# Gated linear attention in blocks of 128 tokens, and two heads or maps at a time in the softmax and stick-breaking attentions

## The chip, the core and the metric

The kernel runs on one core of one Trainium2 chip. The metric is the device time of one execution in microseconds (us); the median of several is given. A core has five engines with their own instruction streams: TensorE (PE, matrix products), VectorE (DVE), ScalarE (ACT), GpSimd (POOL) and SyncE (SP, which starts most transfers here). They wait for each other by semaphores. PE's clock is granted at one of two levels, 1.2 and 2.4 GHz; the profile gives the mean grant of a stretch as a share of the higher one.

## What is computed

Two network blocks in a chain, on 512 tokens of width 1024, all in float32. The first (two layers) has stick-breaking attention (8 heads of 64), differential attention (4 heads, two maps of 64 each), a mixture of experts and a gate. The second has a gated delta network, a gated linear attention, a merge and a lookup of single experts. What the change touches:

```python
def stick_breaking_attention(q, k, v):            # per head, per block of 128 queries
    z = einsum('bhqd,bhkd->bhqk', qb, k) * scale
    strict = key_idx[None, :] < q_idx[:, None]
    log_stay = where(strict, log_sigmoid(-z), 0.0)
    between = cumsum(log_stay, axis=3, reverse=True) - log_stay
    w = where(strict, exp(log_sigmoid(z) + between), 0.0)
    return einsum('bhqk,bhkd->bhqd', w, v)

def differential_attention(q, k, v, lam):         # two maps m per head
    s = einsum('bhmqd,bhmkd->bhmqk', qb, k) * scale
    a = softmax(where(allowed, s, neg), axis=-1)
    return einsum('bhqk,bhkd->bhqd', a[:, :, 0] - lam * a[:, :, 1], v)

def _gla_chunked(q, k, v, logf, s0):              # chunks of 64 tokens; run forwards and backwards
    bc = cumsum(logf, axis=3)
    ref = bc[..., CHUNK // 2:CHUNK // 2 + 1, :]
    scores = einsum('bhnid,bhnjd->bhnij', q * exp(bc - ref), k * exp(ref - bc))
    scores = where(incl, scores, 0.0)
    o_intra = einsum('bhnij,bhnjv->bhniv', scores, v)
    q_dec = q * exp(bc)
    k_dec = k * exp(bc[..., -1:, :] - bc)
    tot = exp(bc[..., -1, :])
    def step(S, xs):
        qd_c, kd_c, v_c, tot_c = xs
        o_c = einsum('bhcd,bhdv->bhcv', qd_c, S)
        S = tot_c[..., :, None] * S + einsum('bhcd,bhcv->bhdv', kd_c, v_c)
        return S, o_c
    s_fin, o_inter = scan(step, s0, (q_dec, k_dec, v, tot))
    return o_intra + o_inter, s_fin
```

The gated linear attention has 8 heads of 128, runs over 256 context tokens first (4 chunks, only the state counts) and then over the 512 tokens (8 chunks), in both directions, and is normed and gated.

## The kernel before

Tiles are 128 partitions by up to 512 columns. PE multiplies a weight tile (rows of weights are contracted, columns of weights become rows of the result) with a moving tile and writes into a bank of 128x512 fp32 in PSUM. A weight tile of 64 rows takes half of the array's rows, one of 64 columns half of its columns. A plain fp32 product runs as two passes, a transpose (against `ident`) as one. Projections by large weights (`proj`, `proj2`) are made of three products of split numbers each (`mm3`, L305 to L311: hi x hi, hi x lo, lo x hi), into `acc`, `acc2` or `acc_c`; the split of a raw weight tile into `w_hi` (ACT) and `w_lo` (DVE or POOL) is L291 to L293 and L1212 to L1213.

The program is written in Python loops; a list scheduler then fixes each engine's order ahead of the run, so products of different steps stand mixed on PE, in an order that does not change at run time. How many tiles of a name live at once is set by pools: `bufs=1` makes the next user wait for the last reader.

*stick* (L566) goes through 8 heads; per head and block of keys `kb` it makes the logits `z` (L581: 64 weight rows, 128 to 512 columns), adds a mask by a product with `ident_b` (L582), takes softplus on ACT and DVE, splits it into `sp_hi` and `sp_lo`, sums over later keys by products with triangles (L597), takes exp into `st_w` and multiplies with `v` into `po` (L601: 64 weight columns; two heads share a bank). *diff* (L609) makes logits `s` (L630, mask L631) of the two maps one after the other, softmax, difference, transposes and `ydif` (L649). Projections of the same layer fill PE between them.

*gla* (L1628) works on four groups `hg` of two heads. It projects q, the two forget gates and v of a group (`proj2`), then per head `j` and direction `d`:

- a cumulative sum `bc` (L1709) of the log gates, in place; `x` and `e1`, the scaled k and q (L1712 to L1719);
- scores of each of 8 chunks into one bank per head that a product with zeros (`zb`, L1702) has cleared: later queries against all 64 keys (L1725), earlier queries against the earlier 32 (L1727); so 16 products a direction, with 32 moving columns each;
- `qd`, `kd`, the totals, and `kd` transposed into `kn` (L1744, copied out by ACT at L1745);
- per chunk in order, 11 of 12 chunks, the state product `kv` (L1758: 64 weight rows, into `pt_kv0` or `pt_kv1` by the chunk's half of its block of 128), and the state update on DVE (L1765, L1767) into `S8`;
- after both directions, a multiply with a mask `le` (L1770), a sum of directions on POOL (L1772), and per chunk three products into `gl_o` (L1776: scores with v; L1777 and L1778: `qd` with the state of each direction), each with 64 weight columns. Then norm, gate, transposes (`pt_o`, L1793) and a split.

The gate projection of a group (`g_ev`) is issued in its first head, the merge gates' projection (`between(hg)`) behind its second. PSUM in this stage: four banks for `acc`, two for `pt`, two for `tr` (`pt_s`, `gl_o`).

Of the kernel before, what the change touches and what calls it, by code (L numbers as in the profile page):

```python
# [20 lines left out]
P = 128  # L21
D = 1024
S = 512
NB = S // P
# [154 lines left out]
class Net:  # L179
# [386 lines left out]
    def stick(self, qT, kT, v, op, pool):  # L566

        nc = self.nc
        res = []
        po = None  # L570
        for h in range(8):
            t, r0 = h // 2, (h % 2) * 64
            rows = slice(r0, r0 + 64)
            if h % 2 == 0:
                po = self.tr("po")
                nc.tensor.matmul(po, self.zero_b[:, :P], self.zero_b, start=True, stop=True)
            sp = [None] * 4
            for kb in (3, 2, 1, 0):
                n = S - kb * P
                z = self.pt("z")[:, :n]  # L580
                nc.tensor.matmul(z, kT[t][rows, kb * P:(kb + 1) * P], qT[t][rows, kb * P:], start=True, stop=False)  # L581
                nc.tensor.matmul(z[:, :P], self.ident_b, self.mask_sb, start=False, stop=True)  # L582
                e = pool.tile([P, S], F32, tag="st_e", name="st_e")[:, :n]
                nc.scalar.activation(out=e, in_=z, func=AF.Abs)
                nc.scalar.activation(out=e, in_=e, func=AF.Exp, scale=-1.0)
                nc.scalar.activation(out=e, in_=e, func=AF.Ln, bias=1.0)
                f = pool.tile([P, S], F32, tag="st_f", name="st_f")[:, :n]
                nc.vector.scalar_tensor_tensor(f, z, 0.0, e, op0=ALU.max, op1=ALU.add)
                hi = pool.tile([P, n], F32R, tag=f"sp_hi{kb}", name="sp_hi")
                lo = pool.tile([P, n], F32R, tag=f"sp_lo{kb}", name="sp_lo")  # L590
                nc.vector.tensor_copy(hi, f)
                nc.vector.tensor_tensor(lo, f, hi.bitcast(F32), op=ALU.subtract)
                sp[kb] = (hi, lo)
                for k2 in range(kb, 4):
                    tri = self.neg_tri if k2 == kb else self.neg_ones
                    for part in range(2):
                        nc.tensor.matmul(z[:, (k2 - kb) * P:], tri, sp[k2][part], start=False,  # L597
                                         stop=True, skip_group_check=True)
                w = pool.tile([P, S], F32, tag="st_w", name="st_w")[:, :n]
                nc.scalar.activation(out=w, in_=z, func=AF.Exp)  # L600
                nc.tensor.matmul(po[rows, kb * P:], v[kb][:, h * 64:(h + 1) * 64], w, start=False,  # L601
                                 stop=True, skip_group_check=True)
            if h % 2 == 1:
                o = op.tile([P, S], F32, tag=f"oa{t}", name=f"oa{t}")
                nc.scalar.copy(o, po)
                res.append(o)
        return res

    def diff(self, i, dn, dv, ap, op, pool, steps):  # L609

        nc = self.nc
# [9 lines left out]
        res = []  # L621
        for h in range(4):
            y = self.tr("ydif")
            for qb in range(NB):
                n = (qb + 1) * P
                es = []
                for m in range(2):
                    rows = slice(64 * m, 64 * m + 64)
                    s = self.pt("s")[:, :n]
                    nc.tensor.matmul(s, T["q"][h][rows, qb * P:(qb + 1) * P], T["k"][h][rows, :n], start=True, stop=False)  # L630
                    nc.tensor.matmul(s[:, n - P:], self.ident_b, self.mask_da, start=False, stop=True)  # L631
                    mx = self.tiny.tile([P, 1], F32, tag=f"mx{m}", name="mx")
# [473 lines left out]
    def masks2(self):  # L1106
# [11 lines left out]

        self.le2 = c.tile([P, 2, P], F32, name="le2")
# [164 lines left out]
    def gdn(self, acts, gp, oa_d):  # L1284
        nc = self.nc
        self.conv = gp.tile([P, 24, 3], F32, name="conv")
# [341 lines left out]
    def gla(self, acts, keep, between):  # L1628
# [8 lines left out]
        with ExitStack() as st:  # L1637
# [6 lines left out]
            zb = gp.tile([P, 1, P], BF16, name="zb2")  # L1644
            nc.gpsimd.memset(zb, 0.0)
            res = []
            for hg in range(4):
# [50 lines left out]
                for j in range(2):  # L1698
                    h = hg * 2 + j
                    Sst, qd = [], []  # L1700
                    sps = self.tr("pt_s")
                    nc.tensor.matmul(sps.rearrange("p (n i) -> p n i", n=4), zb[:, 0], zb.to_broadcast([P, 4, P]),  # L1702
                                     start=True, stop=True)
                    sps = sps.rearrange("p (d b i) -> p d b i", d=2, b=NB)
                    for d in range(2):
# [666 lines left out]
```

## Time and profile before

| | us |
|---|---|
| median of 3 runs | 4505.92 (4497.12 to 4510.54) |
| profiled execution, its own time | 4499.69 |
| its span on the core | 4497.9 |
| PE busy, 21636 instructions | 4207.5 |
| DVE busy | 2759.6 |
| ACT busy | 1669.0 |
| POOL busy | 1137.9 |

The profile is of one execution, on the profiler's clock. Busy times of PE are of pipelined products: a product's shown duration overlaps with its neighbours, so the price of one is read from the distance between starts. Rows of "busy time by stretch" are: start:end, length, then PE, weight load (PEld), DVE, ACT and POOL with busy us and instruction counts, then PE's granted clock, the busy share of the transfer engines and GB/s. Rows by operation give line, engine, operation, output<-inputs, weight rows*columns, moving rows x columns, count, busy time, mean duration in ns, and the idle time before it with what ended most of it. The GLA runs from about 2303 to 2954 us; the attentions of the two layers from about 95 to 345 and from about 905 to 1190 us.

### The profile page before, as it was taken

To read this page: it belongs to the slowest core of one execution; us is meant where nothing else is said; L and a number is where in the kernel's file an instruction comes from. 1 tells how busy PE (TensorE), PEld (TensorE's weight loads), DVE (VectorE), ACT (ScalarE), POOL (GpSimd) and SP (SyncE) were. 2 spreads that over 40 slices of the span, in tenths; PEclk is the share of its full clock that TensorE was granted. 3 is DMA by queue.
4 is the path that set the end of the run, shared out by engine and by line. 5 is a ranking of instruction groups with operands and counts; after the bars stand their busy time and mean duration, and the time that the engine had idled before them with its cause. 6 is when DMAs were issued, how large, how long until landed. Compare 5 with 4: busy or idle time off the path is not lost. (4 is left out here: it accounts for less than half of the span.)

```text
span 4497.9 us, 59856 instructions
## 1 busy us (share of the span) xinstructions
PE 4207.5 (94%) x21636; PEld 3209.9 (71%) x21637; DVE 2759.6 (61%) x6172; ACT 1669.0 (37%) x3160; POOL 1137.9 (25%) x1086
## 2 busy tenths in 40 slices
PE   8999899999989998889999999998889999999998
PEld 6677544767764466777877676676779888988986
DVE  5455455544554564778753544534999777777776
ACT  4544211454421154444433232323346433333333
POOL 2002100100020023222000110214679534343443
PEclk9999999999999998899988898999999999999999
DMA  4144796313459921222211111124135898888875
GB/s 131 36 125 152 287 419 253 112 50 96 131 202 410 411 76 54 53 63 62 62 29 40 31 50 40 38 89 152 59 115 202 278 317 304 294 300 304 286 271 197
DMA packets 342590, 739.77 MB, mean 164 GB/s; under 512 B 72512, under 2 KB 175024, under 8 KB 314640
## 3 DMA queue, kind: packets, MB, share of 16 engines
q1 hardware_dynamic: 277536, 540.54, 36.0%
q0 software_dynamic: 45376, 167.76, 10.2%
q10 hardware_dynamic: 19376, 27.57, 1.7%
q8 instruction: 174, 2.85, 0.3%
q14 instruction: 128, 1.05, 0.1%
HBM read 694.07 MB, written 41.70 MB: 164 GB/s over the span
## 5 line engine op out<-in xcount | busy, mean ns | idle before, releaser
L308 PE MATMUL acc<-rn_hi,w_hi 128*128 128x512 f32 x1224 | 520.4, 426 | 34.3 <-ACT w_hi L1212 16.2
L308 PE MATMUL acc<-rn_hi,w_lo 128*128 128x512 f32 x1224 | 517.9, 424 | 31.5 <-DVE w_lo L1213 12.2
L308 PE MATMUL acc<-rn_lo,w_hi 128*128 128x512 f32 x1224 | 513.3, 419 | 2.0 <-POOL rn_lo L275 2.0
L293 POOL TENSOR_TENSOR w_lo<-w_raw,w_hi 128x512 fp32r<-128x512 f32 x103 | 136.1, 1322 | 1035.5 <-ACT w_hi L291 922.9
L2195 ACT CAST p_hi<-p_raw 128x1024 fp32r<-128x1024 f32 x256 | 268.5, 1049 | 330.9 <-PE pu L308 243.1
L291 ACT CAST w_hi<-w_raw 128x512 fp32r<-128x512 f32 x316 | 196.1, 621 | 516.3 <-PE acc L308 400.0
L308 PE MATMUL pu<-rn_hi,p_lo 128*128 128x384 f32 x1024 | 352.0, 344 | 16.8 <-POOL p_lo L2196 14.4
L308 PE MATMUL pu<-rn_hi,p_hi 128*128 128x384 f32 x1024 | 349.8, 342 | 4.6 <-ACT p_hi L2195 3.5
L308 PE MATMUL pu<-rn_lo,p_hi 128*128 128x384 f32 x1024 | 349.0, 341 | 0.0
L2196 DVE TENSOR_TENSOR p_lo<-p_raw,p_hi 128x1024 fp32r<-128x1024 f32 x243 | 297.1, 1223 | 72.7 <-ACT p_hi L2195 72.7
L293 DVE TENSOR_TENSOR w_lo<-w_raw,w_hi 128x512 fp32r<-128x512 f32 x213 | 151.4, 711 | 272.7 <-ACT w_hi L291 261.4
L308 PEld LDWEIGHTS acc<-rn_hi,w_lo 128*128 128x128 f32 x1224 | 243.5, 199 | 103.7 <-DVE w_lo L1213 16.7
L308 PE MATMUL py<-p_hi,ahi 128*128 128x512 f32 x768 | 304.7, 397 | 6.3 <-ACT ahi L274 3.8
L308 PE MATMUL py<-p_lo,ahi 128*128 128x512 f32 x768 | 304.8, 397 | 1.3 <-DVE p_lo L2196 1.3
L308 PE MATMUL py<-p_hi,alo 128*128 128x512 f32 x768 | 304.9, 397 | 0.0
L308 PEld LDWEIGHTS acc<-rn_hi,w_hi 128*128 128x128 f32 x1224 | 242.5, 198 | 86.3 <-ACT w_hi L1212 19.7
L308 PEld LDWEIGHTS acc<-rn_lo,w_hi 128*128 128x128 f32 x1224 | 242.5, 198 | 44.6 <-issue 4.2
L2185 POOL DMA_INDIRECT eu<-in_expert_v_dram,idx x128 | 189.0, 1477 | 266.9 <-DVE py L2089 250.5
L2185 POOL DMA_INDIRECT eu<-in_expert_u_dram,idx x128 | 179.2, 1400 | 281.7 <-DVE dots L2075 264.4
L956 PE MATMUL gu<-wgu,xe 128*64 128x512 f32 x1024 | 243.3, 600 | 0.0
L308 PEld LDWEIGHTS pu<-rn_hi,p_lo 128*128 128x128 f32 x1024 | 194.8, 190 | 23.6 <-POOL p_lo L2196 17.9
L308 PEld LDWEIGHTS pu<-rn_hi,p_hi 128*128 128x128 f32 x1024 | 195.0, 190 | 10.4 <-ACT p_hi L2195 4.7
(736 smaller groups left out, 9609.2 us busy)
## 6 DMA issues: line engine op xcount, KB each, us to landing
w_raw<-in_w_in_dram SPq DMA_DIRECT2D x336, 256.0 KB, 2.7
p_raw<-in_expert_u_T_dram SPq DMA_DIRECT2D x128, 512.0 KB, 3.6
p_raw<-in_expert_v_dram SPq DMA_DIRECT2D x128, 512.0 KB, 4.9
wgu<-in_w_exp_gate_dram SPq DMA_DIRECT2D x62, 1024.0 KB, 11.8
wgu<-in_w_exp_up_dram SPq DMA_DIRECT2D x62, 1024.0 KB, 14.0
wdn<-in_w_exp_down_dram SPq DMA_DIRECT2D x60, 1024.0 KB, 12.2
ada_w<-in_w_ada_dram SPq DMA_DIRECT2D x96, 256.0 KB, 3.0
gates_d<-gst ACTq DMA_DIRECT2D x24, 1024.0 KB, 4.3
```

The lines of the kernel that those rows point to most:

```text
L291: self.nc.scalar.copy(hi, raw)
L293: eng.tensor_tensor(lo, raw, hi.bitcast(F32), op=ALU.subtract)
L308: self.nc.tensor.matmul(ps, l, r, start=st, stop=sp or shared, skip_group_check=shared)
L956: nc.tensor.matmul(gu[64 * e:64 * e + 64, :], xe[:, c, 64 * e:64 * e + 64], wgu[e][:, :, c, :], start=c == 0, stop=c == KC - 1)
L2185: self.nc.gpsimd.indirect_dma_start(out=t, out_offset=None, in_=rows, in_offset=bass.IndirectOffsetOnAxis(ap=idx, axis=0))
L2195: self.nc.scalar.copy(hi, raw)
L2196: (eng or self.nc.vector).tensor_tensor(lo, raw, hi.bitcast(F32), op=ALU.subtract)
```

## The change

The stick attention takes two heads at a time: both `z` products, both masks, then softplus and weights of each, then both `po`. The differential attention issues the `s` products of both maps together. Four masks that only the delta network uses are built at its start (`masks_gdn`). In the gated linear attention work goes by blocks of 128 tokens (two chunks): scores of a block are two products with 128 weight columns and 2x32 moving columns (the earlier half of keys from `xh`, a shifted copy of `x` in which other places hold values that are not used), and a copy by a mask of integers (`inside`) takes the diagonal 64x64 parts into `sc`, which stays zero elsewhere; `kn` holds each chunk's keys with zeros in the other chunk's rows, so a state product has 128 weight rows, and four share one bank `pt_kv`; the products of scores with v have 128 weight rows and columns, and the products with the states follow, first one column half, then the other.

```diff
@@ stick @@
+        for t in range(4):
+            po = self.tr("po")
...
+                zs = [self.pt("z")[:, :n] for _ in halves]
+                for z, rows in zip(zs, halves):
+                    nc.tensor.matmul(z, kT[t][rows, kb * P:(kb + 1) * P], qT[t][rows, kb * P:], start=True, stop=False)
+                for z in zs:
+                    nc.tensor.matmul(z[:, :P], self.ident_b, self.mask_sb, start=False, stop=True)
...
+                    sp[r][kb] = (hi, lo)
...
+                for r, rows in enumerate(halves):
+                    h = 2 * t + r
+                    nc.tensor.matmul(po[rows, kb * P:], v[kb][:, h * 64:(h + 1) * 64], ws[r], start=False,
+                                     stop=True, skip_group_check=True)
@@ diff @@
-                for m in range(2):
+                both = [self.pt("s")[:, :n] for _ in range(2)]
+                for m, s in enumerate(both):
                     rows = slice(64 * m, 64 * m + 64)
-                    s = self.pt("s")[:, :n]
                     nc.tensor.matmul(s, T["q"][h][rows, qb * P:(qb + 1) * P], T["k"][h][rows, :n], start=True, stop=False)
+                for s in both:
                     nc.tensor.matmul(s[:, n - P:], self.ident_b, self.mask_da, start=False, stop=True)
@@ gla @@
-            zb = gp.tile([P, 1, P], BF16, name="zb2")
-            nc.gpsimd.memset(zb, 0.0)
+            inside = gp.tile([P, 2, P], I32, name="inside")
...
+            sc = gp.tile([P, 2, NB, P], F32, name="gl_sc")
+            kn = gp.tile([P, 6, 2, P], F32, name="gl_kn")
+            xh = gp.tile([P, 32 + 8 * 64], F32, name="gl_xh")
+            for t in (sc, kn, xh):
+                nc.gpsimd.memset(t, 0.0)
...
-                        for c in range(8):
-                            p0 = 64 * (c % 2)
-                            nc.tensor.matmul(sps[p0:p0 + 64, d, c // 2, ilate], x[:, c, :], e1[:, c, ilate],
-                                             start=False, stop=True, skip_group_check=True)
-                            nc.tensor.matmul(sps[p0 + early.start:p0 + early.stop, d, c // 2, early], x[:, c, early],
-                                             e1[:, c, early], start=False, stop=True, skip_group_check=True)
+                        nc.vector.tensor_copy(xh[:, 32:].rearrange("p (c i) -> p c i", c=8)[:, :, 0:32], x[:, :, early])
+                        xf = xh[:, 32 - early.start:][:, :S]
+                        sps = self.tr("pt_s").rearrange("p (b i) -> p b i", b=NB)
+                        for b in range(NB):
+                            cs = slice(2 * b, 2 * b + 2)
+                            s2 = sps[:, b].rearrange("p (c i) -> p c i", c=2)
+                            nc.tensor.matmul(s2[:, :, ilate], x[:, cs].rearrange("p c i -> p (c i)"), e1[:, cs, ilate],
+                                             start=True, stop=True)
+                            nc.tensor.matmul(s2[:, :, early], xf[:, b * P:(b + 1) * P], e1[:, cs, early],
+                                             start=True, stop=True)
+                        nc.vector.copy_predicated(out=sc[:, d], mask=inside[:, d:d + 1].to_broadcast([P, NB, P]), data=sps)
...
+                        ends = tp.tile([P, 12, 1], F32, tag="ends", name="gl_ends", bufs=1)
+                        nc.vector.tensor_copy(ends, bc[:, :, last:last + 1])
...
+                        kd = bc
...
-                            nc.scalar.copy(kn[:, b0:b0 + nb], pt[:, :nb * P].rearrange("p (b c) -> p b c", c=P))
+                            for hf in range(2):
+                                nc.scalar.copy(kn[H[hf], b0:b0 + nb, hf], pt[H[hf], :nb * P].rearrange("p (b c) -> p b c", c=P))
...
-                                nc.tensor.matmul(pt[:, n * P:(n + 1) * P], kn[cs, c // 2, :], v[cs, c // 2, j * P:(j + 1) * P],
-                                                 start=True, stop=True)
+                                nc.tensor.matmul(kv, kn[:, c // 2, c % 2, :], v[:, c // 2, j * P:(j + 1) * P], start=True, stop=True)
...
-                    tt(sc, sps, self.le.unsqueeze(2).to_broadcast([P, 2, NB, 64]), op=ALU.mult)
-                    ss = tp.tile([P, NB, 64], F32, tag="scs", name="gl_scs", bufs=1)
+                    ss = tp.tile([P, 768], F32, tag="vT", name="gl_scs", bufs=1)[:, :512].rearrange("p (b i) -> p b i", b=NB)
...
-                    for c in range(8):
-                        cs, b = H[c % 2], c // 2
-                        nc.tensor.matmul(o[cs, b, :], ss[cs, b, :], v[cs, b, j * P:(j + 1) * P], start=True, stop=False)
-                        nc.tensor.matmul(o[cs, b, :], qd[0][:, c, :], Sst[0][:, c, :], start=False, stop=False)
-                        nc.tensor.matmul(o[cs, b, :], qd[1][:, c, :], Sst[1][:, c, :], start=False, stop=True)
+                    for b in range(NB):
+                        nc.tensor.matmul(o[:, b, :], ss[:, b, :], v[:, b, j * P:(j + 1) * P], start=b == 0, stop=True, skip_group_check=True)
+                    for b in range(NB):
+                        for d in range(2):
+                            for c in (2 * b, 2 * b + 1):
+                                nc.tensor.matmul(o[H[c % 2], b, :], qd[d][:, c, :], Sst[d][:, c, :], start=False, stop=True,
+                                                 skip_group_check=True)
```

The scheduler's order on PE, in the first heads phase of the GLA. State products of the second direction of the first head before the change (`acc` are projection products, `pt_kv` state products; numbers behind names tell tiles apart):

```order
L308 MATMUL acc_20574<-rn_hi_13383,w_hi_20597 128x512
L1758 MATMUL pt_kv1_20206<-glv_19923,gl_kn_20182 128x128
L308 MATMUL acc_20574<-rn_lo_13384,w_hi_20597 128x512
L308 MATMUL acc_20574<-rn_hi_13383,w_lo_20598 128x512
L308 MATMUL acc_20575<-rn_hi_13383,w_hi_20597 128x512
L308 MATMUL acc_20575<-rn_lo_13384,w_hi_20597 128x512
L1758 MATMUL pt_kv0_20205<-glv_19923,gl_kn_20182 128x128
L308 MATMUL acc_20575<-rn_hi_13383,w_lo_20598 128x512
L1758 MATMUL pt_kv1_20206<-glv_19923,gl_kn_20182 128x128
L308 MATMUL acc_20576<-rn_hi_13383,w_hi_20597 128x512
```

and after it:

```order
L1782 MATMUL pt_kv_20199<-glv_19931,gl_kn_19572 128x128
L308 MATMUL acc_20537<-rn_hi_13371,w_lo_20562 128x512
L308 MATMUL acc_20538<-rn_hi_13371,w_hi_20561 128x512
L1782 MATMUL pt_kv_20190<-glv_19931,gl_kn_19572 128x128
L308 MATMUL acc_20538<-rn_lo_13372,w_hi_20561 128x512
L308 MATMUL acc_20538<-rn_hi_13371,w_lo_20562 128x512
L308 MATMUL acc_20539<-rn_hi_13371,w_hi_20561 128x512
L1782 MATMUL pt_kv_20190<-glv_19931,gl_kn_19572 128x128
L308 MATMUL acc_20539<-rn_lo_13372,w_hi_20561 128x512
```

Each state product now writes a bank shared by four, and stands alone among projection products as most did before; with 128 weight rows its place in a row half is gone.

Scores of the second direction of the first head before (L1725 later queries, L1727 earlier ones; sixteen in all, one state product among them):

```order
L1758 MATMUL pt_kv1_20122<-glv_19923,gl_kn_20108 128x128
L1725 MATMUL pt_s_20073<-gl_e1_20152,gl_x_20150 64x32
L1727 MATMUL pt_s_20073<-gl_e1_20152,gl_x_20150 32x32
L1725 MATMUL pt_s_20073<-gl_e1_20152,gl_x_20150 64x32
L1727 MATMUL pt_s_20073<-gl_e1_20152,gl_x_20150 32x32
L1725 MATMUL pt_s_20073<-gl_e1_20152,gl_x_20150 64x32
L1727 MATMUL pt_s_20073<-gl_e1_20152,gl_x_20150 32x32
```

and after, with both directions of the head next to each other (L1747 and L1749):

```order
L308 MATMUL acc2_20260<-rn_hi_13371,w_lo_20282 128x512
L1749 MATMUL pt_s_20090<-gl_e1_20084,gl_xh_19573 128x2x32
L1747 MATMUL pt_s_20090<-gl_e1_20084,gl_x_20082 128x2x32
L1749 MATMUL pt_s_20090<-gl_e1_20084,gl_xh_19573 128x2x32
L1747 MATMUL pt_s_20090<-gl_e1_20084,gl_x_20082 128x2x32
L1749 MATMUL pt_s_20090<-gl_e1_20084,gl_xh_19573 128x2x32
L1747 MATMUL pt_s_20090<-gl_e1_20084,gl_x_20082 128x2x32
L1749 MATMUL pt_s_20090<-gl_e1_20084,gl_xh_19573 128x2x32
L1747 MATMUL pt_s_20157<-gl_e1_20151,gl_x_20149 128x2x32
L308 MATMUL acc2_20259<-rn_hi_13371,w_hi_20299 128x512
```

Sixteen small products became eight, and transposes of `kd` and projections stand between the sets.

Outputs of the first head before (L1776 scores with v, L1777 and L1778 the states):

```order
L308 MATMUL acc_20574<-rn_hi_13383,w_lo_20616 128x512
L1778 MATMUL gl_o_20227<-gl_S_20193,gl_qd_20173 64x128
L1776 MATMUL gl_o_20227<-glv_19923,gl_scs_20225 64x128
L1777 MATMUL gl_o_20227<-gl_S_20119,gl_qd_20099 64x128
L1778 MATMUL gl_o_20227<-gl_S_20193,gl_qd_20173 64x128
L1776 MATMUL gl_o_20227<-glv_19923,gl_scs_20225 64x128
L1777 MATMUL gl_o_20227<-gl_S_20119,gl_qd_20099 64x128
L1778 MATMUL gl_o_20227<-gl_S_20193,gl_qd_20173 64x128
```

and after (L1795 scores with v, L1799 the states; x2 are two products on the two column halves):

```order
L1795 MATMUL gl_o_20217<-glv_19931,gl_scs_20215 128x128 x4
...
L308 MATMUL acc_20539<-rn_hi_13371,w_lo_20598 128x512
L1799 MATMUL gl_o_20217<-gl_S_20189,gl_qd_20167 64x128 x2
L1799 MATMUL gl_o_20217<-gl_S_20122,gl_qd_20100 64x128 x2
L1799 MATMUL gl_o_20217<-gl_S_20189,gl_qd_20167 64x128 x2
L1799 MATMUL gl_o_20217<-gl_S_20122,gl_qd_20100 64x128 x2
L1799 MATMUL gl_o_20217<-gl_S_20189,gl_qd_20167 64x128 x2
```

The four full products stand some eighty rows ahead of the run of products with the states, which alternates between the column halves; before, three products in turn wrote the same half.

## Rows read from the trace of the kernel before

**Rows 1.** The page: busy time of each engine, share of the span, instructions.

```profile
PE 4207.5 (94%) x21636; PEld 3209.9 (71%) x21637; DVE 2759.6 (61%) x6172; ACT 1669.0 (37%) x3160; POOL 1137.9 (25%) x1086
```

**Rows 2.** Busy time by stretch, stick and diff (columns as said above).

```profile
95.00:240.00 145.00, 144.63 (x633) 95.06 (x632) 55.82 (x129) 76.47 (x171) 7.86 (x7) 1.00 0.18 50
...
1050.00:1190.00 140.00, 136.27 (x635) 98.50 (x634) 83.19 (x198) 61.01 (x140) 10.36 (x8) 0.99 0.44 119
```

**Rows 3.** The same view, the GLA whole and three stretches of it.

```profile
2303.80:2953.90 650.10, 616.88 (x2993) 439.24 (x2993) 301.01 (x527) 192.77 (x300) 90.41 (x60) 0.88 0.14 39
...
2303.00:2428.00 125.00, 119.04 (x517) 78.42 (x517) 60.53 (x118) 31.55 (x52) 15.44 (x12) 0.78 0.11 32
2428.00:2494.00 66.00, 59.84 (x316) 50.56 (x314) 32.67 (x33) 28.93 (x42) 15.21 (x8) 0.95 0.21 56
...
2858.00:2954.00 96.00, 93.19 (x487) 61.58 (x488) 46.06 (x103) 20.95 (x36) 9.77 (x8) 0.95 0.11 31
```

**Rows 4.** The same view, one heads phase cut at its runs.

```profile
2358.80:2365.70 6.90, 6.90 (x45) 4.36 (x44) 0.00 (x0) 0.03 (x1) 0.00 (x0) 1.00 0.05 16
2375.60:2378.90 3.30, 3.30 (x34) 2.64 (x33) 1.64 (x3) 1.57 (x4) 1.28 (x1) 1.00 0.03 11
2379.00:2382.30 3.30, 3.30 (x13) 2.17 (x14) 0.32 (x2) 0.89 (x2) 1.27 (x1) 0.50 0.00 0
...
2385.80:2406.20 20.40, 20.40 (x53) 12.30 (x52) 5.79 (x13) 2.09 (x4) 0.73 (x1) 0.50 0.05 13
```

**Rows 5.** The same view, first and last of the four group borders.

```profile
2298.00:2314.00 16.00, 8.30 (x30) 5.70 (x29) 15.55 (x18) 8.73 (x14) 7.42 (x7) 0.68 0.11 44
...
2836.00:2847.00 11.00, 5.51 (x23) 4.22 (x22) 11.00 (x8) 6.72 (x12) 10.31 (x6) 0.69 0.15 36
```

**Rows 6.** PE by operation and shape in the GLA (xcount | busy, mean).

```profile
L1758 PE MATMUL pt_kv<-glv,gl_kn 64*128 64x128 f32 x352 | 86.1, 367 | 0.0
...
L1702 PE MATMUL pt_s<-zb 128*128 128x512 bf16 x8 | 3.6, 447 | 1.2 <-DVE g_gt L1595 1.2
```

**Rows 7.** Timeline of PE, kv alone (start, duration, operation, passes).

```profile
2354.04 0.50 PE L308 MATMUL acc<-rn_hi,w_hi 128*128 128x512 f32 x1
2354.47 0.48 PE L1758 MATMUL pt_kv<-glv,gl_kn 64*128 64x128 f32 x2
2354.89 0.50 PE L308 MATMUL acc<-rn_lo,w_hi 128*128 128x512 f32 x1
```

**Rows 8.** Timeline of PE, four 128x128 products, then projections.

```profile
270.08 1.08 PE L649 MATMUL ydif<-dv,da_t 128*128 128x128 f32 x8
270.92 0.48 PE L308 MATMUL acc<-rn_hi,w_lo 128*128 128x512 f32 x1
271.23 0.39 PE L308 MATMUL acc<-rn_hi,w_hi 128*128 128x512 f32 x1
271.46 0.39 PE L308 MATMUL acc<-rn_lo,w_hi 128*128 128x512 f32 x1
```

**Rows 9.** Timeline of PE, one 128x128 product alone, and the next.

```profile
249.45 0.49 PE L649 MATMUL ydif<-dv,da_t 128*128 128x128 f32 x2
249.78 0.22 PE L631 MATMUL s<-mask_da,ident_b 128*128 128x128 bf16 x1
```

**Rows 10.** Timeline of PE, two kv in different row halves.

```profile
2348.84 0.49 PE L1758 MATMUL pt_kv<-glv,gl_kn 64*128 64x128 f32 x4
```

**Rows 11.** Timeline of PE, po of two heads together, of one alone.

```profile
114.49 1.07 PE L601 MATMUL po<-st_w,v 128*64 128x512 f32 x4
...
126.98 1.07 PE L601 MATMUL po<-st_w,v 128*64 128x512 f32 x2
```

**Rows 12.** DVE by operation and shape in the GLA.

```profile
L1767 DVE SCALAR_TENSOR_TENSOR gl_S<-gl_S,gl_tot,pt_kv 128x128 f32<-128x128 f32 x112 | 38.8, 346 | 71.5 <-PE pt_kv L1758 70.7
...
L1770 DVE TENSOR_TENSOR gl_sc<-pt_s,le 128x512 f32<-128x512 f32 x8 | 5.5, 691 | 27.8 <-PE pt_s L1727 27.8
```

**Rows 13.** Waits of PE in the GLA (us in total, times, longest).

```profile
PE pt_o L1793 <- DVE gl_y L1788: 8.4, 4, 2.2
```

More of the change, by code (lines that the diff above doesn't have):

```diff
@@ L569, in stick @@
         res = []
[L570 to L577, printed above, removed]
+        halves = (slice(0, 64), slice(64, 128))
+        for t in range(4):
+            po = self.tr("po")
+            nc.tensor.matmul(po, self.zero_b[:, :P], self.zero_b, start=True, stop=True)
+            sp = [[None] * 4 for _ in halves]
@@ L578, in stick @@
             for kb in (3, 2, 1, 0):
                 n = S - kb * P
[L580 to L600, printed above, removed]
@@ new lines, in stick @@
+                for z in zs:
+                    nc.tensor.matmul(z[:, :P], self.ident_b, self.mask_sb, start=False, stop=True)
+                ws = []
+                for r, z in enumerate(zs):
+                    e = pool.tile([P, S], F32, tag="st_e", name="st_e")[:, :n]
+                    nc.scalar.activation(out=e, in_=z, func=AF.Abs)
+                    nc.scalar.activation(out=e, in_=e, func=AF.Exp, scale=-1.0)
+                    nc.scalar.activation(out=e, in_=e, func=AF.Ln, bias=1.0)
+                    f = pool.tile([P, S], F32, tag="st_f", name="st_f")[:, :n]
+                    nc.vector.scalar_tensor_tensor(f, z, 0.0, e, op0=ALU.max, op1=ALU.add)
+                    hi = pool.tile([P, n], F32R, tag=f"sp_hi{kb}", name="sp_hi")
+                    lo = pool.tile([P, n], F32R, tag=f"sp_lo{kb}", name="sp_lo")
+                    nc.vector.tensor_copy(hi, f)
+                    nc.vector.tensor_tensor(lo, f, hi.bitcast(F32), op=ALU.subtract)
+                    sp[r][kb] = (hi, lo)
+                    for k2 in range(kb, 4):
+                        tri = self.neg_tri if k2 == kb else self.neg_ones
+                        for part in range(2):
+                            nc.tensor.matmul(z[:, (k2 - kb) * P:], tri, sp[r][k2][part], start=False,
+                                             stop=True, skip_group_check=True)
+                    w = pool.tile([P, S], F32, tag="st_w", name="st_w", bufs=3)[:, :n]
+                    nc.scalar.activation(out=w, in_=z, func=AF.Exp)
+                    ws.append(w)
@@ L607, in stick @@
+                for r, rows in enumerate(halves):
+                    h = 2 * t + r
+                    nc.tensor.matmul(po[rows, kb * P:], v[kb][:, h * 64:(h + 1) * 64], ws[r], start=False,
+                                     stop=True, skip_group_check=True)
+            o = op.tile([P, S], F32, tag=f"oa{t}", name=f"oa{t}")
+            nc.scalar.copy(o, po)
+            res.append(o)
         return res
@@ L626, in diff @@
                 es = []
-                for m in range(2):
+                both = [self.pt("s")[:, :n] for _ in range(2)]
+                for m, s in enumerate(both):
                     rows = slice(64 * m, 64 * m + 64)
-                    s = self.pt("s")[:, :n]
                     nc.tensor.matmul(s, T["q"][h][rows, qb * P:(qb + 1) * P], T["k"][h][rows, :n], start=True, stop=False)
+                for s in both:
                     nc.tensor.matmul(s[:, n - P:], self.ident_b, self.mask_da, start=False, stop=True)
+                for m, s in enumerate(both):
                     mx = self.tiny.tile([P, 1], F32, tag=f"mx{m}", name="mx")
@@ L1117, in masks2, with masks_gdn @@
                                         base=0, channel_multiplier=-sgn)
+    def masks_gdn(self, c):
+        nc = self.nc
         self.le2 = c.tile([P, 2, P], F32, name="le2")
```

35 lines of the change are left out of this document (11 added, 24 removed).

## Prediction

> **What bounds the kernel now.** I read the page's busy shares first: TensorE (PE) works 94% of the span [rows 1], so a change pays where PE has less to do or stops less. Busy times by stretch then separate the two places that the change touches. In the stick-breaking and differential attentions PE is busy 144.63 of 145 us and 136.27 of 140, at granted clock 1.00 and 0.99, with VectorE (DVE) and ScalarE (ACT) at 83 us or less [rows 2]: those are plain sums of PE work. The gated linear attention (GLA) is the long one: 650.1 us from its first projection to its last transpose, PE busy 616.88, mean granted clock 0.88 [rows 3]. It alternates: four heads phases (125, 107, 107 and 96 us, 435 together), in which the small products of two heads run between projection products, and three stretches of pure projection (66, 75 and 75 us, clock 0.95).
>
> Where the clock falls is seen in one heads phase cut fine [rows 4]. During a run of output products it is 1.00, during a run of sixteen score products too, but just behind such a run it is 0.50 (the lower of the two levels, 1.2 of 2.4 GHz), for 3.3 us once and for 20.4 us the next time. What else is low lies at the four group borders, three of 11 us and one of 16, at 0.68 to 0.69 with PE busy about half [rows 5]: there PE waits for split weights.
>
> So the GLA's 650.1 us split into 33.2 us of idle PE (650.10 less 616.88), a loss to the clock of 0.12 x 650 = 78 us (156 us at the lower level, each losing half), and 539 us of work at full clock. Of the 156 us, the 49 us of border at about 0.685 make 31; some 125 are left, which I put down to the score runs.
>
> **The change part by part.** An fp32 product is two PE passes in the trace (x2 is one product).
>
> *State products (kv).* 352 passes, 176 products, with 64 rows of weights [rows 6]. Now 54 of them stand as 27 pairs in different row halves and 122 alone between projection products. A lone one: projection at 2354.04, kv at 2354.47, next projection at 2354.89 [rows 7], so 0.85 us for the two, where projections by themselves start 0.23 apart (271.23 to 271.46 in [rows 8]): it costs 0.62. After, it has 128 rows and stands alone. A run of four such products took 270.08 to 270.92, 0.21 each, and the projection behind it 0.31 instead of 0.23 [rows 8]: 0.29 in all. One alone, behind a 64-row product, held its place for 0.33 [rows 9]: 0.41 in all, the dear end. Each of the 122 saves 0.21 to 0.33: 26 to 40 us. The 27 pairs gain nothing: two kv in different halves last 0.49 [rows 10], as one does [rows 7], which is about two of the new ones. I stay near the run, since projections with 128 rows surround it: **-36**.
>
> *Scores.* 16 runs of 3.3 us [rows 4] become 16 sets of 8 products with 128 weight columns and 64 moving columns. At the 0.21 of the 128-column product a set costs 1.7 us, so 16 x 1.6 = **-25**; at 0.31 each, the price of a half-width output today, it is -13. The eight zeroing products go: **-4** [rows 6].
>
> *Outputs.* 22 of a head's 24 products fill the 6.9 us [rows 4]: 0.31 each, 7.5 for 24. After: four full products (0.84) and sixteen of 64 weight columns that alternate between the two column halves. Two products on different column halves lasted as long as one in the stick attention (1.07 us for four passes and for two [rows 11]), so I take a pair at the 0.43 of a kv pair: 3.4, in all 4.3 a head, 8 x 3.2 = **-26**. If they do not lie side by side they keep 0.31 each: 5.8 a head, -14.
>
> Together -91: 539 becomes 448 us of work at full clock.
>
> *Clock.* If no set of scores ends in the lower level any more, 62 of the 78 us come back and the borders' 16 stay: **-62**. The ends are 0 and 62. I take 62, because a set is half as long with full weights, and because the run of 22 outputs, twice as long as a score run, kept 1.00 [rows 4].
>
> *DVE, ACT, POOL.* Per head and direction DVE gets a 128x256 copy (half of a 128x512 row's 0.69 [rows 12]), a small copy of end values (under 0.3) and a copy by mask of 128x512, between 0.69 and twice that; it loses one 0.69 multiply a head. That is 4 to 7 us more a group. ACT writes kn in halves (two more short copies), POOL's add is twice as wide. All of it costs nothing while PE's work covers it: a heads phase shrinks from 435/4 = 109 us to 109 - (91 + 62)/4 = 71, and DVE needs 46 to 61 there today [rows 3], 50 to 68 after. That cover is thin. If it goes, the chain of the 22 state updates a head (0.35 each [rows 12]), which follow the kv products one by one, is what PE waits for, and kn, xh and each state set have one buffer. Today's waits of this kind are small: 8.4 us in four waits for the normed output [rows 13]. I add **+15** for late links (ends 0 and 60) and **+10** at the end of the last heads phase, where the new order has no projection left between the last outputs and their transposes (21 of them, 5 us, cover that wait now) and the last eight kv stand in a row with a state update between each. The 33 us of idle elsewhere stay.
>
> GLA after: 448 + 33 + 16 + 25 = 522, so **-128**.
>
> *Stick and diff.* Six pairs of z products and thirteen pairs of s products, none before, now stand side by side in different row halves. The second of a pair is then free: 0.42 us for the ten that have 128 columns, and for the nine with two or three times the columns an estimated 1.6 times that: 4 + 6 = 10. Of the po products nine pairs lay side by side, now four, but the second was narrow in most: +1. A pair of heads now fills both softplus buffers at once, so the next pair's first softplus waits for this pair's last products; DVE and ACT have 57 us or more free there [rows 2], and projections stand between. **-9**, ends -18 and +15. Building four masks moves from the start into the second block, some 2 us on POOL: 0, ends +-2.
>
> **Sum:** -128 - 9 = -137. The profiled execution took 4499.69 us (span 4497.9), 6 under the median of 4505.92; I put the saving against the median: 4505.9 - 137 = 4369, rounded to **4370**.
>
> **The rivals.**
>
> *A, as above:* 4345 to 4395, chance 0.55.
>
> *B, the clock keeps falling.* The new sets are still runs of few moving columns. For it: the level is low behind both score runs that I cut out. Against it: the output run keeps 1.00. All 62 us stay: 4432. 0.12.
>
> *C, wide rows gain nothing.* If a 128-row product took the 0.42 us of a 64-row one, the lone kv would save nothing and the 27 pairs, which share their time now, would lose 0.42 each: the term goes from -36 to +11, 4417. Against it stands 0.21 for each of four 128-row products [rows 8]. 0.05. The Trainium skill has this rule: TensorE: Matmul & The Clock Gate, section "Why this matters for your kernels", says that a single K=32 product takes the same time as one of K=128 and that small K gains only when tiles run side by side. By that rule this part of the change gives the pairs away for nothing; the trace agrees on pairs (0.49 against 0.48) and differs on the lone product (0.42 against 0.21).
>
> *D, the dear prices:* kv 26, scores 13, outputs 14 instead of 36, 25, 26: +34, 4404. 0.10.
>
> *E, DVE bounds the heads phases.* DVE is busy 61% over the whole span [rows 1]. If its steps, which wait for PE, ACT and POOL in turn, let it be no busier in a heads phase, its 50 to 68 us need 82 to 111 us where the sum has 77 (71 and a quarter of 25): +20 to +136, mostly 4395 to 4460. For it: the one buffer of kn, xh and the states. Against it: today PE and not the chain fills the phase (busy 119.04 of 125 and 93.19 of 96 [rows 3]). 0.13.
>
> *F, the other side: heads phases as long as now or longer.* The mechanism is E's, with the two directions of a head laid end to end by those single buffers. It decides at a phase of 109 + 9/4 = 111 us (no change in all) and at 115 us (0.3% slower). DVE would then stand still half of the time. 4500 to 4540; 0.05, the larger part slower.
>
> **How the numbers follow.** The time is A's. The three runs shown differ by 13 us (4497.12 to 4510.54), so 0.3%, or 13.5 us, is about what can be told from no change. Above, the range leaves out F, the upper part of E and little of B (0.13 in all); below, what would come without the 25 us of new waits and with stick and diff at -18 is 4336, and a little less if the border idle shrinks too (0.06): **4325 to 4440**. Faster 0.93 (all but F and E's end), same 0.03, slower 0.04.
>
> **What would show it.** The GLA stretch should last 510 to 540 us at a mean granted clock of about 0.96; the stretch behind a set of scores should show 1.00 (0.50 is B). A lone kv among projections should hold PE for 0.21 to 0.33 us (0.42 is C), a pair of half-width outputs in different column halves 0.43 (0.62 is D). PE's idle in the GLA should be near 58 us; over 90 with DVE named as releaser is E. In stick and diff together each layer should be 4 to 5 us shorter. The prediction is wrong if PE's work falls as summed and the stage does not: then the chain of DVE, ACT and POOL steps sets the heads phase, which I sized at 15 us.

## The result, and the profile after

The changed kernel takes 4381.05 us (median of 4, 4378.97 to 4384.84) against 4505.65 us: ratio 0.9726, interval 0.9710 to 0.9743. That is 125 us less; 137 were predicted, and the time lies in the range of 4325 to 4440, 11 us above the point. One execution in all the runs below, of the kernel with only the state products old, took 13180.68 us and is left out of every figure. The profiled execution took 4381.8 us with a span of 4379.9, 118 us less than the span before.

The page's busy times of the changed kernel (as [rows 1]):

```profile
PE 4054.2 (93%) x21308; PEld 3139.6 (72%) x21309; DVE 2778.6 (63%) x6214; ACT 1683.9 (38%) x3192; POOL 1150.9 (26%) x1089
```

PE lost 153 us of busy time, more than the span: part of the gain went into waits. Busy time by stretch of the changed kernel: the whole GLA, and in one heads phase two sets of scores (from 2368 and from 2372) and what stands behind them.

```profile
2304.40:2835.30 530.90, 472.32 (x2679) 380.86 (x2678) 315.36 (x570) 213.19 (x338) 99.81 (x61) 0.94 0.19 53
2368.00:2372.00 4.00, 3.56 (x26) 2.98 (x24) 2.72 (x5) 3.88 (x7) 1.13 (x1) 1.00 0.15 51
2372.00:2376.00 4.00, 4.00 (x30) 3.62 (x29) 2.84 (x8) 2.89 (x4) 0.00 (x0) 1.00 0.07 10
2376.00:2396.00 20.00, 18.46 (x106) 14.11 (x106) 9.71 (x25) 6.50 (x11) 1.27 (x1) 1.00 0.18 51
```

Against [rows 3] the stage is 119 us shorter (650.1 to 530.9; 128 predicted): all of the 118 us of span. Behind the scores the clock stays at 1.00, where [rows 4] had 0.50 for up to 20 us. The first three rows below are the prediction's account: idle is length less PE busy, the clock's loss is one less the mean grant, times the length, and work is what is left. It subtracts idle time at the lower level twice, once as idle and once as the clock's loss. The last two rows are summed from the same view over stretches of 1 us and take the clock's loss on PE's busy time alone:

| | idle | lost to the clock | work at full clock |
|---|---|---|---|
| before, 650.1 us | 33 | 78 | 539 |
| predicted, 522 | 58 | 16 | 448 |
| measured, 530.9 | 59 | 32 | 440 |
| before, clock on busy time | 33 | 74 | 543 |
| measured, clock on busy time | 59 | 20 | 452 |

So work fell by 91 us and the clock's loss by 54, and idle grew by 25.

The timeline of PE in the changed kernel, state products alone among projections, then a run of 14 half-width output products (28 passes):

```profile
2342.05 0.40 PE L308 MATMUL acc<-rn_hi,w_hi 128*128 128x512 f32 x1
2342.29 0.39 PE L1782 MATMUL pt_kv<-glv,gl_kn 128*128 128x128 f32 x2
2342.43 0.48 PE L308 MATMUL acc<-rn_lo,w_hi 128*128 128x512 f32 x1
2342.75 0.39 PE L308 MATMUL acc<-rn_hi,w_lo 128*128 128x512 f32 x1
...
2351.43 1.75 PE L1799 MATMUL gl_o<-gl_S,gl_qd 128*64 128x128 f32 x28
2353.11 0.50 PE L308 MATMUL acc<-rn_hi,w_hi 128*128 128x512 f32 x1
```

The lone state product here, like most of those around it, holds PE for 0.14 us (2342.29 to 2342.43) and makes the next projection 0.09 dearer (0.32 instead of 0.23): 0.23 against 0.62 before [rows 7]. Fourteen outputs take 1.68 us, 0.12 each, against 0.31 [rows 4].

The waits of PE in the stage (as [rows 13]):

```profile
PE acc L308 <- DVE w_lo L1223: 12.8, 6, 3.6
PE pt_o L1815 <- DVE gl_y L1810: 12.6, 6, 4.6
PE pt_kv L1782 <- DVE gl_S L1788: 6.0, 9, 1.2
PE pt_v L1716 <- DVE glv L1717: 5.9, 1, 5.9
PE acc L308 <- ACT w_hi L1222: 5.8, 3, 1.9
PE gl_o L1795 <- POOL gl_scs L1791: 3.4, 7, 0.6
```

The wait for the normed output grew from 8.4 to 12.6 us, 4.6 of it at the very end of the stage; the waits of a state product for the update ahead of it (6.0) and of the outputs for POOL's sum of scores (3.4) are new. The transposes of v wait 5.9 us for DVE's copy; before, they waited 3.3 us for ACT (`PE pt_v L1695 <- ACT gl_vT L1690: 3.3, 1, 3.3`).

DVE by operation in the stage, the three operations that are new:

```profile
L1751 DVE COPY_PREDICATED gl_sc<-inside,pt_s 128x512 f32<-128x512 int32 x16 | 11.9, 745 | 9.8 <-PE pt_s L1749 9.7
L1741 DVE COPY gl_xh<-gl_x 128x256 f32<-128x256 f32 x16 | 8.4, 524 | 0.1
L1757 DVE COPY gl_ends<-gl_lf 128x12 f32<-128x12 f32 x16 | 4.5, 282 | 3.4 <-ACT gl_tot L1759 3.4
```

The copy by mask costs what the multiply did (0.745 against 0.69 [rows 12]), the lower end of what was allowed for.

### The profile page after: what moved, and what is told of

Read it like the earlier page. It is cut to its first block, busy times and chain, and to the rows that moved or that the text cites. A ratio compares the mean times of both kernels' runs of the same rounds, so it can differ in the third digit from the quotient of the medians.

```text
span 4379.9 us, 59166 instructions
## 1 busy us (share of the span) xinstructions
PE 4054.2 (93%) x21308; PEld 3139.6 (72%) x21309; DVE 2778.6 (63%) x6214; ACT 1683.9 (38%) x3192; POOL 1150.9 (26%) x1089
## 5 line engine op out<-in xcount | busy, mean ns | idle before, releaser
L308 PE MATMUL acc<-rn_hi,w_lo 128*128 128x512 f32 x1224 | 506.1, 414 | 36.9 <-DVE w_lo L1223 13.1
L308 PE MATMUL acc<-rn_hi,w_hi 128*128 128x512 f32 x1224 | 506.9, 415 | 32.3 <-ACT w_hi L1222 16.9
L308 PE MATMUL acc<-rn_lo,w_hi 128*128 128x512 f32 x1224 | 500.7, 409 | 2.0 <-POOL rn_lo L275 2.0
```

The costliest lines, as they stand in the source:

```text
L308: self.nc.tensor.matmul(ps, l, r, start=st, stop=sp or shared, skip_group_check=shared)
```

## The experiments

The three groups of products of the GLA (state products, scores, outputs) were each put back alone and each kept alone, the attentions were put back and kept alone, and in one kernel all three groups are old. Ratios are to the kernel before on the same chip.

**The attentions.** First the changed kernel with the old `stick` and `diff` (both functions as in the kernel before), then the kernel before with the new ones.

> The changed kernel with stick and diff put back to their old form. Theory 1 (what the two traces show: 5 us less PE work there, given back as 4 us of longer waits for split weights): the attentions are worth nothing, about 4381 us, 4376 to 4386, as the changed kernel. Rival (the predicted term): worth 9 us, so about 4390.

Measured: 4380.84 us, ratio 0.9718 (0.9694 to 0.9742).

> The kernel before with the new stick and diff only. Theory 1: 4505 us, no change (4499 to 4509), PE work in the two attentions about 4 to 5 us smaller and PE's idle there as much larger. Rival (the predicted term): 4497 us.

Measured: 4499.95 us, ratio 0.9985 (0.9969 to 1.0001): too wide to tell 0 from 9 us by itself. The first run speaks for 0: without the new attentions the median is 0.2 us lower. So does the kernel with all three groups old, further below, which has the new attentions and gains nothing. What happened to their gain is seen in the busy times of six matching stretches from the start of the attentions to the routing in both layers. The kernel before, then the changed one:

```profile
sum 809.40, PE 783.79 PEld 563.48 DVE 404.88 ACT 378.25 POOL 87.53; mean PE 130.63 PEld 93.91 DVE 67.48 ACT 63.04 POOL 14.59
```

```profile
sum 808.90, PE 779.53 PEld 557.92 DVE 406.70 ACT 377.50 POOL 87.96; mean PE 129.92 PEld 92.99 DVE 67.78 ACT 62.92 POOL 14.66
```

PE works 4.3 us less, and the stretches last 0.5 us less: the rest is idle. In the first layer the longest item is PE's wait for split weights, with the new attentions and (in the kernel of the first experiment) with the old ones:

```profile
PE acc L308 <- DVE w_lo L293: 8.0, 3, 5.1
```

```profile
PE acc L308 <- DVE w_lo L293: 3.3, 3, 1.5
```

So in the first layer the work saved ahead of a projection is waited away in front of it: the weights' split did not come earlier. And not each pair ran side by side. The two `s` products of 128 columns that come first in the changed kernel took 0.81 us, as two in turn, while the first two `z` products took 0.43:

```profile
246.69 0.88 PE L635 MATMUL s<-dkT,dqT 64*128 64x128 f32 x4
247.50 0.28 PE L637 MATMUL s<-mask_da,ident_b 128*128 128x128 bf16 x2
...
100.07 0.49 PE L580 MATMUL z<-q,k 64*128 64x128 f32 x4
100.50 0.28 PE L582 MATMUL z<-mask_sb,ident_b 128*128 128x128 bf16 x2
```

The first `s` pair of the second layer took 0.81 us as well; of the 19 pairs these two are the only ones that ran in turn. Why they did was not tried.

**One group of products new.** Each kernel is the changed one with two groups put back.

State products new; scores (sixteen products into a cleared bank, and a multiply with the mask into the diagonal parts of `sc`) and outputs old:

```diff
-                            nc.tensor.matmul(s2[:, :, ilate], x[:, cs].rearrange("p c i -> p (c i)"), e1[:, cs, ilate],
-                                             start=True, stop=True)
...
+                            nc.tensor.matmul(sps[p0:p0 + 64, d, c // 2, ilate], x[:, c, :], e1[:, c, ilate],
+                                             start=False, stop=True, skip_group_check=True)
...
+                        nc.tensor.matmul(o[cs, b, :], ss[cs, b, cs], v[cs, b, j * P:(j + 1) * P], start=True, stop=False)
+                        nc.tensor.matmul(o[cs, b, :], qd[0][:, c, :], Sst[0][:, c, :], start=False, stop=False)
+                        nc.tensor.matmul(o[cs, b, :], qd[1][:, c, :], Sst[1][:, c, :], start=False, stop=True)
```

> The changed kernel with the old scores (sixteen products into a cleared bank) and the old order and form of the outputs, so of the three groups of products only the state products are new. Theory 1 (the clock falls behind runs of score products): the clock's share stays lost; 122 lone state products save 0.3 to 0.4 us each, 36 to 49 in all, so 4455 to 4470 us, mean granted clock of the GLA about 0.87, 0.50 behind each run of scores. Theory 2 (the clock falls because of the half-array state products between projections): 62 us more come back, about 4400 us, clock 0.95.

Measured: 4463.18 us, ratio 0.9904 (0.9879 to 0.9928), 45 us less than before, in the range of theory 1. The stage by stretch:

```profile
2305.50:2919.80 614.30, 564.18 (x3003) 430.00 (x3002) 299.96 (x551) 212.23 (x337) 98.50 (x61) 0.90 0.17 46
```

Scores new; state products and outputs old (the state products by the lines of the next diff, put back):

> The changed kernel with the old state products (64 weight rows, two banks) and the old outputs, so only the scores are new. Theory 1: scores save 25, the clearing products 4, the clock 62, together about 91: 4405 to 4425 us, clock of the GLA about 0.95 and nowhere 0.50 behind the scores. Theory 2: 29 us only, about 4475 us, clock 0.88.

Measured: 4442.60 us, ratio 0.9851 (0.9826 to 0.9877), 66 us less, between the two theories. The execution profiled here is the slowest of four, 4458.70 us, and its mean grant the lowest (0.963 against 0.966 to 0.970). The stage, then a stretch with a set of scores and four 64-row state products, two among the scores and two behind them, and what follows it:

```profile
2312.20:2913.30 601.10, 556.68 (x2738) 410.10 (x2737) 306.45 (x569) 210.81 (x335) 95.15 (x61) 0.93 0.17 46
2651.00:2655.00 4.00, 4.00 (x27) 3.17 (x25) 1.57 (x4) 1.52 (x4) 0.34 (x1) 1.00 0.00 0
2655.10:2672.20 17.10, 17.10 (x46) 10.65 (x45) 3.47 (x10) 3.34 (x7) 0.83 (x1) 0.50 0.06 16
```

Theory 1 said that the clock would nowhere be 0.50 behind new scores. Here it is, for 17.1 us, and once more, as long, in the last heads phase (from 2825). In this execution new scores alone do not keep the clock up everywhere.

Outputs new; scores and state products old:

> The changed kernel with old scores and old state products, so only the outputs are new. Theory (outputs alone save 31 to 37 us of work and leave the falls of the clock behind the score runs where they were, near 157 us at the lower level): 4470 to 4480 us against 4509. Rival (the half-width outputs had their part in the low clock): below 4460 us.

Measured: 4465.30 us, ratio 0.9900 (0.9879 to 0.9920), 45 us less, between theory and rival: these products have a part in the low clock, but a small one (12 us in the table below). The stage:

```profile
2311.40:2920.80 609.40, 571.53 (x2936) 422.06 (x2935) 299.85 (x550) 210.40 (x334) 96.35 (x60) 0.89 0.17 45
```

**One group old.** State products:

```diff
-                                kv = pt[:, n]
-                                nc.tensor.matmul(kv, kn[:, c // 2, c % 2, :], v[:, c // 2, j * P:(j + 1) * P], start=True, stop=True)
+                                kv, cs = pts_[c % 2][:, n], H[c % 2]
+                                nc.tensor.matmul(kv, kn[cs, c // 2, c % 2, :], v[cs, c // 2, j * P:(j + 1) * P], start=True, stop=True)
```

> The changed kernel with the old state products alone (64 weight rows, two banks). Theory 1 (a lone 64-row product costs 0.62 us and keeps the clock low where it is low, a 128-row one 0.22): 49 us of price and some 15 to 20 of clock come back on top of 4381, so 4430 to 4455 us; in the trace the low clock behind scores mixed with such products, as in the run with only new scores. Rival (the rule that wide rows gain nothing): 4370 to 4385 us.

Measured: 4412.36 us (three executions), ratio 0.9797 (0.9773 to 0.9821), 31 us more than the changed kernel, less than theory 1 said and far from the rival. Every fall of the clock in this trace stands behind idle of PE and none behind scores, so that part of theory 1 fell:

```profile
2312.50:2869.50 557.00, 512.84 (x2667) 389.68 (x2665) 308.66 (x569) 209.54 (x332) 99.27 (x60) 0.95 0.18 49
```

Scores old:

> The changed kernel with the old scores alone. Theory 1: 29 us of work and the falls of the clock behind the score runs return, short ones since no half-array state products stand behind them (some 60 us at the lower level, so 30 of time): 4430 to 4450 us. Rival (with full state products and outputs the score runs no longer lower the clock): 4410 us.

Measured: 4421.14 us, ratio 0.9816 (0.9797 to 0.9836), 40 us more than the changed kernel, again between. The stage, then a run of old scores and the two stretches behind it:

```profile
2311.60:2879.10 567.50, 516.90 (x2939) 405.46 (x2938) 304.37 (x551) 211.39 (x337) 98.57 (x61) 0.92 0.18 49
2474.00:2477.60 3.60, 3.60 (x37) 2.90 (x36) 1.36 (x4) 1.09 (x1) 0.00 (x0) 1.00 0.44 129
2477.70:2487.90 10.20, 10.20 (x47) 7.89 (x46) 2.50 (x4) 1.90 (x4) 1.27 (x1) 0.50 0.01 2
2488.00:2500.00 12.00, 12.00 (x70) 9.32 (x69) 5.15 (x14) 2.55 (x6) 0.00 (x0) 1.00 0.17 45
```

The fall behind old scores returns, but it ends after 10.2 us; in the kernel before one lasted at least 20.4 [rows 4].

Outputs old:

> The changed kernel with the old outputs alone (24 products of 64 weight columns a head). By the trace of the changed kernel 14 half-width products took 1.68 us, 0.12 each, and full ones 0.22, so a head costs 2.8 instead of 7.5 us: 37 us come back, 4410 to 4425 us. Rivals: the predicted term, 26 us, 4407; the dear price, 14 us, 4395. The granted clock should not be lowered by these runs.

Measured: 4418.20 us, ratio 0.9808 (0.9787 to 0.9828), 37 us more than the changed kernel, as the trace's price of 0.12 said.

```profile
2308.90:2874.90 566.00, 508.93 (x2742) 395.75 (x2740) 307.77 (x570) 212.59 (x337) 98.31 (x61) 0.94 0.19 50
```

All three old:

> The changed kernel with all three groups of products old: what is left of the change are the new stick and diff, the padded copies of kn, kd in place, the shared slot of the running state and the wider sum. Theory 1: these are worth nothing, 4495 to 4515 us. Rival (part of the gain is theirs): below 4490 us.

Measured: 4510.81 us, ratio 1.0007 (0.9990 to 1.0023): nothing of the gain is in the copies, the shared slot or the wider sum.

```profile
2308.40:2966.90 658.50, 618.12 (x3003) 442.44 (x3002) 303.32 (x551) 214.40 (x337) 97.91 (x61) 0.88 0.16 42
```

The same account for all of them, with the clock's loss on PE's busy time alone, summed over stretches of 1 us of the profiled execution:

| new groups | length | idle | lost to the clock | work |
|---|---|---|---|---|
| none | 658.5 | 40 | 75 | 543 |
| state products | 614.3 | 50 | 56 | 509 |
| scores | 601.1 | 44 | 32 | 525 |
| outputs | 609.4 | 38 | 63 | 508 |
| all but state products | 557.0 | 44 | 21 | 492 |
| all but scores | 567.5 | 51 | 42 | 474 |
| all but outputs | 566.0 | 57 | 23 | 486 |
| all three | 530.9 | 59 | 20 | 452 |

Work adds up: alone the groups save 35, 19 and 35, together 91. The clock does not: alone they return 19, 43 and 12, which makes 74, and all three return 55. With new scores and one other group new the loss is at 21 to 23, as good as with all three; with old scores it stays at 42.

The row of new scores comes from their slowest execution. Each execution's span and mean grant are on record, so the clock's loss over the whole program can be estimated for all of them (one less the grant, times the span; the last digit of the grant is worth 4 to 5 us). The medians are 198 to 203 us for the kernel before, 147 for the changed kernel, 147 for new scores alone (133 to 165, the profiled one) and 170 with only the scores old. By this estimate new scores alone return about all that the three groups return, and the two other groups without them some two thirds of it. The gains overlap, and that is most of why the three together gain 125 us where the sum of each alone is 45 + 66 + 45 = 156.

**A version that beats both.** The changed kernel has no projection left at the end of the last heads phase. In two versions the projections for the merge gates come later, so that two of the four stand behind the last group (the second version is shown; the first has none behind group 0 and one each behind groups 1 and 2):

```diff
-                between(hg)
+                for n in ((0,), (), (1,), (2, 3))[hg]:
+                    between(n)
```

> The changed kernel with the projections for the merge gates issued one group later (none behind group 0, two behind the last), so that 21 projection products again stand between the last outputs and their transposes and some between the last state products. Theory (the idle of the tail, some 8 us, and the lower clock behind it, 20 us that lose half, are paid because no projection is left there): 4365 to 4374 us against 4381, and no 0.50 in the tail of the stage. Rival (the filler is only missing elsewhere afterwards): 4378 to 4384.

> The same with the projection behind group 0 kept and none behind group 1. Theory: as the kernel before it, 4365 to 4374 us. Rival: 4378 to 4384.

Measured: 4363.94 us, ratio 0.9676 (0.9659 to 0.9694), and 4362.55 us, ratio 0.9670 (0.9653 to 0.9688): some 18 us faster than the changed kernel, a little more than the theory's range. The end of the stage in the changed kernel (timeline of PE):

```profile
2827.69 2.35 PE L1799 MATMUL gl_o<-gl_S,gl_qd 128*64 128x128 f32 x20
2834.64 1.12 PE L1815 MATMUL pt_o<-ident,gl_y 128*128 128x128 f32 x4 [4.60 <-DVE gl_y L1810]
```

and in the second version, with its stage by stretch:

```profile
2813.54 0.40 PE L308 MATMUL acc<-rn_lo,w_hi 128*128 128x512 f32 x1
2813.77 0.40 PE L308 MATMUL acc<-rn_hi,w_lo 128*128 128x512 f32 x1
2814.20 0.66 PE L1815 MATMUL pt_o<-ident,gl_y 128*128 128x128 f32 x4
```

```profile
2311.40:2814.60 503.20, 452.35 (x2630) 365.21 (x2629) 309.48 (x566) 206.47 (x329) 97.58 (x59) 0.96 0.19 52
```

The wait of 4.60 us is gone and the transposes take 0.66 us (at full clock) instead of 1.12. The stage's loss to the clock, on busy time, is 12 us against 20 and its idle 51 against 59; the stage is shorter by 28 us because 11 us of work moved behind its end, too.

## Why the prediction was right, and where it was off

**What bounds the stage** (a sum of PE work, the clock, few waits) held: the three terms make up the 119 us.

**The work at full clock** was predicted at -91 and measured at -91, but the parts were not: two errors cancel, which is luck. State products: -36 predicted; -35 alone and -40 undone (492 - 452). Scores with the clearing products: -29 predicted; -19 alone, -22 undone. Why they saved less was not tried. Outputs: -26 predicted; -35 alone, -33 undone: I priced a pair on two column halves at the 0.43 of a kv pair on two row halves, and it costs 0.24.

**The clock** was predicted at -62 and measured at -54 on busy time (-46 in the prediction's own count). The mechanism held in the main. In the trace before, each of the ten falls away from the group borders begins in or just behind a run of at least sixteen old score products; in the changed kernel every low stretch stands behind some idle of PE. New scores alone return 43 us in their slowest execution, and by the estimate from all four about as much as the whole change. But the prediction put all of it down to the score runs, and the other products take part: with old scores among full state products and new outputs the falls are shorter and some 33 us return without new scores, and among 64-row state products and old outputs new scores can still end in the lower level (17.1 us at 0.50 in the row above). What kept the 46 from being 62 is something else: 16 us of loss were to stay at the borders, and 32 stayed. Of some 60 us at the lower level in the changed kernel, 41 stand at the four borders (31 before), 12 in the tail and 7 behind waits in two heads phases. The 25 us of new waits that I allowed for came (33 to 59 us of idle), and I did not charge them for the clock that they cost. Why the borders are low for longer was not tried.

**The new waits** were sized right as a sum (25, measured 25) and in their place at the end: with projections there the stage lost 8 us of idle and 8 us of clock. Most of the rest are waits of state products for the update (6.0), of outputs for the sum of scores (3.4) and of the transposes of v in the first group (5.9 against 3.3).

**Stick and diff** is the term that failed: -9 predicted, 0 measured. PE's work fell by 4.3 us instead of 9, and what it saved it spent idle instead, in the first layer mostly in front of split weights. The pairs were counted right, 19, and 17 of them ran side by side; the two that did not explain 0.8 us, and where the rest of the 9 went is not shown. The factor of 1.6 for wider products had no row behind it; a lone one of 256 columns held PE for 0.63 us, 1.5 times the 0.42. I had read these stretches as plain sums of PE work because PE was busy 144.63 of 145 us; the projections behind them are not such a sum.

**The rivals.** B, the clock keeps falling: no, 1.00 behind the scores. C, wide rows gain nothing: no. With only the state products old the kernel takes 4412.36 us, where C has it no slower than 4385, and a lone 128-row product holds PE for 0.14 us where a 64-row one held it for 0.42. The Trainium skill's rule (TensorE: Matmul & The Clock Gate, "Why this matters for your kernels": a K=32 product takes as long as one of K=128) is not what this trace shows for a product that stands alone among full ones; the measurement decides. D, the dear prices: not for state products, which came out at the predicted term, nor for outputs, which came out beyond it; the scores lie between the two (15 to 18 us without the 4 of the clearing products, against 25 and 13). E, DVE bounds the heads phases: only in the small waits above; DVE's work in the stage rose only from 301 to 315 us.

The saving counts 137 predicted against 118 in the spans: 9 us are the attentions and 9 the GLA. The medians differ by 125, since the execution profiled before lay 6 us under its median and the one after does not.

## What to carry to other kernels

Price a small product by the distance between starts in the place where it will stand: among full 128x128 products one that is padded to all rows may cost a third of one that fills half of them. Where several kinds of small products stand in one stretch with a low clock, their shares of the clock overlap: changing one kind can return most of it, so do not add the parts up, and look at the grants of several executions before you call a share. Work taken from PE shows as time only where what PE does next is ready earlier; look at the wait behind the stretch, and keep some full products for the end of a stage in which chains run.

## What the runs showed of the chip that I had not expected

A lone fp32 product with 128 weight rows held PE for 0.14 us between projections; one with 64 rows 0.42 [rows 7]. Fourteen half-width products that alternate between column halves cost 0.12 each, half of a full one (0.21 [rows 8]), so two on two column halves cost about one full product, while two on two row halves cost two (0.43 for the `z` pair above).

The clock fell to 0.50 behind stretches in which PE was busy all the time: behind 3.30 of 3.30 us of old scores [rows 4], 3.60 of 3.60 with full state products around them, and 4.00 of 4.00 with new scores among 64-row state products. The Trainium skill tells of falls behind idle time (TensorE: Matmul & The Clock Gate, "HAM oscillation — how this bites in real kernels"); those are seen here too, at the group borders [rows 5], but PE need not be idle for the level to fall. How much of which kind of product it takes was not tried.
